# The last expert's way out: scattering through four row groups of the array, and a final norm straight from PSUM

## The chip, the cores and the metric

One Trainium2 chip, one of its NeuronCores. The metric is the time of one execution on the device in microseconds; each time below is the median of several executions. The engines that matter are TensorE (PE; PEld is its weight load), VectorE (DVE), ScalarE (ACT), GpSimd (POOL) and SyncE (SP), which issues nearly all DMAs.

## The reference

A two-layer trunk over x of 256 tokens x 1024 features in float32. Each layer is a mixer (a linear recurrence beside a stick-breaking attention) and then a channel mixer with a residual add: a dense SwiGLU in layer 0, and in layer 1 eight experts of width 3072, of which each token takes two. A norm closes the trunk. What the change touches is the end of layer 1:

```python
def swiglu(h, w_g, w_u, w_d):
    return (jax.nn.silu(h @ w_g) * (h @ w_u)) @ w_d

# moe_swiglu: each expert's rows, weighted by the token's gate, are added at the token's place
y = jnp.zeros_like(hf).at[row_tok].add(y_rows * row_gate[:, None])
...
x = x + moe_swiglu(h, router_w[j], moe_w_gate[j], moe_w_up[j], moe_w_down[j])
return rms_norm(x, final_norm)      # x / sqrt(mean(x^2) + 1e-6) * final_norm
```

## The kernel before

x stays in SBUF as two tiles `xs[0]` and `xs[1]` of 128 tokens x 1024. The experts run one after another (`order`, `run`), each with room for `n` tiles of 32 tokens: three tiles (96 tokens) for the five experts with the most tokens, two for the others. The last expert in the order has three. A product (`Expert.product`) reads its weights in four slabs of 1 MB, and holds the tokens stationary: an output tile of 32 tokens x 1024 columns is computed as four column groups of the array, 32 columns each, so that the quarter `q` of the 1024 output columns lands on PSUM partitions `32q` to `32q+32`. A tile is thus 128 partitions x 256, and two tiles share a PSUM bank. Products are `g`, `u` and `d` (gate, up, down), each cut in three (`ES`); the order for the last expert ends g2, u2, d1, d2.

Rows of an expert come from x and go back to it through a 0/1 matrix (`oh`, tokens x slots). `turn_one_hot` turns it by two bf16 transposes in the product u2. After d2, `rows` copies each 32x256 piece from PSUM to its place in `y` (slots x 1024), `scatter` multiplies by the turned one-hot (96 slots in the rows of the array), and VectorE adds the result, times the gate, to `xs`. For the last expert this is done in three rounds over the columns (`THIRDS`: 512, 256, 256), and `Final.square` follows each round with ScalarE's sum of squares, so that the norm's statistics grow with x. `Final.finish` then makes the two reciprocal roots on GpSimd (lines 260, 261), scales each half of each token block (ScalarE line 1148, VectorE line 1149), and SP stores the four halves of 256 KB (lines 1150, 1151).

While this stretch is made, `order_as_written` keeps PE, DVE and ACT in the order of the text; POOL and SP are ordered by the scheduler. PSUM accesses of two engines to one bank are kept apart by semaphores.

Behind it stand two branches (lines 1239, 1240), one behind the other, for an expert that has more tokens than its room: each engine loads one number (line 1238) and jumps over a body with a loop over all experts. With these inputs neither body runs. The arm that is taken instead waits for what is under way on each engine, SP for its stores. Line 1337 is the program's end: SP's last waits and the barrier of all engines.

Of the kernel before, what the change touches and what calls it, by code (L numbers as in the profile page):

```python
# [7 lines left out]
F32 = mybir.dt.float32  # L8
# [44 lines left out]
def trunk(ctx, tc, x, mix_norm, w_in, conv_w, conv_b, w_rgate, b_rgate, w_igate, b_igate, lru_lambda,  # L53
# [860 lines left out]
    def moe(j, pool, psum, route):  # L914
# [77 lines left out]
        class Expert:  # L992
# [15 lines left out]
            def product(self, name, s, hooks):  # L1008
# [4 lines left out]
                for i in range(4):  # L1013
                    w = load([self.source(name, s)[:, 2 * i:2 * i + 2]])
                    for kk in range(2):
                        k = 2 * i + kk
                        first = k == 0 and (name != "d" or s == 0)
                        last = k == KC - 1 and (name != "d" or s == ES - 1)
                        for t in range(self.n):
                            if name == "d":  # L1020
                                sh = self.turned[s][:, t, kk, i]
                            else:
                                sh = self.xT[:, k, t * 32:(t + 1) * 32]
                            for q in range(QN):
                                PE.matmul(outs[t][q * 32:(q + 1) * 32], sh,  # L1025
                                          w[:, kk * D + q * QW:kk * D + (q + 1) * QW],
                                          start=first and t % 2 == 0,
                                          stop=last and (t % 2 == 1 or t == self.n - 1))
# [56 lines left out]
            def turn_one_hot(self, exact=False):  # L1085
# [7 lines left out]
                if exact:  # L1093
                    self.y = pool.tile([CAP, D], F32, tag="yhi", name="yx", bufs=1)[:c32]
                else:
                    self.yhi = pool.tile([CAP, D], F32R, tag="yhi", name="yhi", bufs=1)[:c32]
                    self.ylo = pool.tile([CAP, D], F32R, name="ylo", bufs=1)[:c32]
# [25 lines left out]
        THIRDS = ((0, 512), (512, 768), (768, 1024))  # L1123

        class Final:
# [8 lines left out]
            def square(self, n, tb):  # L1134
                lo, hi = THIRDS[n]
                ss, x, y = self.ss[tb], xs[tb], self.ys[tb]
                ACT.activation(y[:, 512:512 + hi - lo], x[:, lo:hi], AF.Square, scale=1.0 / 32.0,
                               accum_out=ss[:, n:n + 1])
                if n == 0:
                    POOL.tensor_tensor(y[:, :512], x[:, :512], self.grow[0], op=OP.mult)  # L1140
                if n == 1:
                    POOL.tensor_tensor(ss[:, 0:1], ss[:, 0:1], ss[:, 1:2], op=OP.add)

            def finish(self):
                rs = [rstd_of_halves(ss[:, 0:1], ss[:, 2:3]) for ss in self.ss]
                for tb in range(NB):
                    y0, y1 = self.ys[tb][:, :512], self.ys[tb][:, 512:]
                    ACT.activation(y0, y0, AF.Copy, scale=rs[tb])
                    DVE.scalar_tensor_tensor(y1, xs[tb][:, 512:], rs[tb], self.grow[1], op0=OP.mult, op1=OP.mult)
                    nc.sync.dma_start(out[0, tb * P:(tb + 1) * P, :512], y0)  # L1150
                    nc.sync.dma_start(out[0, tb * P:(tb + 1) * P, 512:], y1)
# [15 lines left out]
        def run(jobs, whole):  # L1167

            waiting = []

            def hooks(name, job, s, i):
# [5 lines left out]
                if name == "u" and s == ES - 1:  # L1177
                    if i == 0 and after:
                        after.one_hot()
                    if i == 2:  # L1180
                        job.turn_one_hot(after is None)
# [9 lines left out]
            final = None  # L1191
            for name, job, s in order(jobs):
                if name == "d" and s == ES - 1 and job is jobs[-1] and whole:
                    final = Final()
# [3 lines left out]
                job.product(name, s, hooks)  # L1198
# [9 lines left out]
            for n, (lo, hi) in enumerate(THIRDS):  # L1208
                for q in range(lo // QW, hi // QW):
                    job.rows(q)  # L1210
                for tb in range(NB):
                    job.scatter(tb, lo, hi)
                if whole:
# [127 lines left out]
```

## Time and profile before

| | |
|---|---|
| median of 3 executions | 1204.24 us (1203.52 to 1204.24) |
| profiled execution, its own time | 1204.76 us |
| span of the profiled execution, first to last instruction | 1202.9 us |
| busy share of the span | PE 96%, PEld 65%, DVE 33%, ACT 27%, POOL 7% |
| mean granted TensorE clock | 0.986 of full speed |
| last down product, last instruction starts | 1176.6 us |
| first and last store issue on SP | 1190.94 us, 1194.34 us |

All times in rows are counted from the span's first instruction. A matmul in float32 is two instructions. The ends of matmuls are modelled and they overlap, so a busy TensorE is not one at its peak, and the pace of a stream is read from the starts. "Idle before, releaser" says how long an engine stood before an instruction and what ended that.

### The profile page before, as it was taken

What the parts mean: (1) busy time and instruction counts of PE and PEld (TensorE: products, weight loads), DVE (VectorE), ACT (ScalarE), POOL (GpSimd) and SP (SyncE); (2) the same over time, 40 slices, a digit from 0 to 9 for tenths busy, and PEclk for the clock granted to TensorE, in tenths of its full rate; (3) what the DMA queues carried; (4) which work ended last, traced back from release to release, by engine and by line L of the source; (5) the groups of instructions that cost most, each with busy time, mean ns of one, the idle gap of its engine ahead of it and who ended that gap; (6) DMA issues with size and microseconds to landing.
All of it is one profiled execution on the core that took longest, in us unless ns stands there. A gap on an engine that the chain in (4) does not pass through costs nothing.

```text
span 1202.9 us, 33274 instructions
## 1 busy us (share of the span) xinstructions
PE 1150.5 (96%) x15027; PEld 786.8 (65%) x15027; DVE 393.0 (33%) x668; ACT 320.6 (27%) x552; POOL 87.5 (7%) x142
## 2 busy tenths in 40 slices
PE   7989999999999979999999999999999999999993
PEld 5978888888898756665565665555565665555651
DVE  5796654555688662002002002011003002002002
ACT  6664644444467551001001001010001001001002
POOL 3154000000003600000000000000000000000001
PEclk9999999999999989999999999999999999999996
DMA  9933655555362289999999999999999999999971
GB/s 279 335 105 105 210 186 198 176 181 185 134 218 89 89 326 409 408 407 407 407 408 407 408 408 408 407 406 405 404 403 404 403 407 399 408 402 403 406 284 40
DMA packets 117032, 375.13 MB, mean 312 GB/s; under 512 B 6032, under 2 KB 22528, under 8 KB 116880
## 3 DMA queue, kind: packets, MB, share of 16 engines
q1 hardware_dynamic: 116592, 372.33, 80.9%
q8 instruction: 122, 2.00, 0.7%
q0 software_dynamic: 288, 0.56, 0.2%
q14 instruction: 30, 0.25, 0.1%
HBM read 371.81 MB, written 1.05 MB: 310 GB/s over the span
## 4 chain that ended last, share of the span: by engine, by line
PE 57%; DMA 3%; DVE 3%; ACT 1%; issue 0%; POOL 0%; POOLq 0%; ACTq 0%
PE d L1025 17%; PE g L1025 17%; PE u L1025 16%; DMA raw<-in_moe_w_up 2%; DMA raw<-in_moe_w_down 2%; PE gat L1076 1%; DVE ylo L1111 1%; PE at L1053 1%; ACT yhi L1110 1%; PE sc L1118 1%; PE sc L1119 1%; PE sc L1116 0%; PE po L148 0%; PE po L147 0%; PE po L149 0%
## 5 line engine op out<-in xcount | busy, mean ns | idle before, releaser
L1025 PE MATMUL u<-raw,xT 128*32 128x256 f32 x4032 | 228.0, 380 | 0.6 <-DMA raw<-in_moe_w_up 0.6
L1025 PE MATMUL g<-raw,xT 128*32 128x256 f32 x4032 | 227.2, 380 | 0.0
L1025 PE MATMUL d<-raw,aT 128*32 128x256 f32 x4032 | 225.5, 379 | 1.3 <-DMA raw<-in_moe_w_down 1.3
L1025 PEld LDWEIGHTS u<-raw,xT 128*32 128x32 f32 x4032 | 127.9, 110 | 89.4 <-issue 5.5
L1025 PEld LDWEIGHTS d<-raw,aT 128*32 128x32 f32 x4032 | 129.2, 110 | 87.3 <-DMA raw<-in_moe_w_down 2.7
L1025 PEld LDWEIGHTS g<-raw,xT 128*32 128x32 f32 x4032 | 127.6, 110 | 87.9 <-issue 6.7
L133 DVE TENSOR_TENSOR wlo<-raw,whi 128x1024 fp32r<-128x1024 f32 x96 | 116.8, 1224 | 93.1 <-ACT whi L132 93.0
L132 ACT ACTIVATE whi<-raw 128x1024 fp32r<-128x1024 f32 x96 | 100.6, 1060 | 106.9 <-PE u L149 38.6
L1058 ACT ACTIVATE aT<-at 128x512 f32<-128x512 f32 x24 | 14.3, 598 | 370.9 <-PE at L1053 354.8
L1040 DVE TENSOR_TENSOR act<-act,u 128x512 f32<-128x512 f32 (+1 forms) x39 | 21.4, 581 | 207.6 <-PE u L1025 146.6
L147 PE MATMUL proj<-hhi,whi 128*128 128x256 f32 x256 | 76.3, 298 | 0.0
L1111 DVE TENSOR_TENSOR ylo<-d,yhi 32x256 fp32r<-32x256 f32 x72 | 30.2, 419 | 133.7 <-ACT yhi L1110 132.9
L148 PE MATMUL proj<-hlo,whi 128*128 128x256 f32 x256 | 73.5, 287 | 0.0
L149 PE MATMUL proj<-hhi,wlo 128*128 128x256 f32 x256 | 73.4, 287 | 0.0
L1140 POOL TENSOR_TENSOR raw<-x,raw 128x512 f32<-128x512 f32 x2 | 2.5, 1270 | 741.5 <-DVE x L1120 741.5
L147 PEld LDWEIGHTS proj<-hhi,whi 128*128 128x128 f32 x256 | 50.1, 196 | 2.0 <-issue 1.5
L148 PEld LDWEIGHTS proj<-hlo,whi 128*128 128x128 f32 x256 | 50.2, 196 | 0.2
L149 PEld LDWEIGHTS proj<-hhi,wlo 128*128 128x128 f32 x256 | 50.1, 196 | 0.0
L1110 ACT ACTIVATE yhi<-d 32x256 fp32r<-32x256 f32 x72 | 27.0, 376 | 78.1 <-PE d L1025 58.3
L1034 ACT ACTIVATE act<-g 128x512 f32<-128x512 f32 (+1 forms) x39 | 18.4, 513 | 98.8 <-PE g L1025 98.8
L143 DVE TENSOR_TENSOR wlo<-raw,whi 128x1024 fp32r<-128x1024 f32 x32 | 39.9, 1254 | 5.2 <-ACT whi L142 5.1
L142 ACT ACTIVATE whi<-raw 128x1024 fp32r<-128x1024 f32 x32 | 33.8, 1061 | 20.7 <-PE proj L148 10.7
(259 smaller groups left out, 1344.2 us busy)
## 6 DMA issues: line engine op xcount, KB each, us to landing
raw<-in_moe_w_gate SPq DMA_DIRECT2D x96, 1024.0 KB, 19.3
raw<-in_moe_w_up SPq DMA_DIRECT2D x96, 1024.0 KB, 18.4
raw<-in_moe_w_down SPq DMA_DIRECT2D x96, 1024.0 KB, 18.5
raw<-in_w_in SPq DMA_DIRECT2D x18, 1024.0 KB, 5.3
raw<-in_dense_w_gate SPq DMA_DIRECT2D x12, 1024.0 KB, 5.2
raw<-in_dense_w_up SPq DMA_DIRECT2D x12, 1024.0 KB, 5.2
raw<-in_dense_w_down SPq DMA_DIRECT2D x12, 1024.0 KB, 5.0
raw<-in_w_out SPq DMA_DIRECT2D x8, 1024.0 KB, 11.4
```

The lines of the kernel that those rows point to most:

```text
L132: ACT.activation(hi, r, AF.Copy)
L133: DVE.tensor_tensor(lo, r, hi.bitcast(F32), op=OP.subtract)
L142: ACT.activation(h3, r, AF.Copy)
L143: DVE.tensor_tensor(lo.rearrange("p (k f) -> p k f", f=P), r, h3.bitcast(F32), op=OP.subtract)
L147: PE.matmul(ps, sh, mh, start=start, stop=False)
L148: PE.matmul(ps, sh, ml, start=False, stop=False)
L149: PE.matmul(ps, sl, mh, start=False, stop=stop)
L1025: PE.matmul(outs[t][q * 32:(q + 1) * 32], sh, w[:, kk * D + q * QW:kk * D + (q + 1) * QW], start=first and t % 2 == 0, stop=last and (t % ...
L1034: ACT.activation(a[:, at], b, AF.Silu)
L1040: DVE.tensor_tensor(a[:, at], a[:, at], b, op=OP.mult)
L1110: ACT.activation(self.yhi[to, w], ps, AF.Copy)
L1111: DVE.tensor_tensor(self.ylo[to, w], ps, self.yhi[to, w].bitcast(F32), op=OP.subtract)
```

## The change

Six things are changed at the end of layer 1, for the last expert alone.

- `spread` replaces the last expert's `turn_one_hot`: VectorE multiplies the one-hot by the gate and repeats each tile's 32 slots four times; six f32 transposes (three for each token block) give a stationary matrix of 128 rows, in which each group of 32 rows holds one tile's slots. ScalarE and VectorE copy it out of PSUM.
- `carry` adds, after each of the four slabs of the last down product, two identity matmuls that put one quarter of the columns of x (both token blocks, 256 columns each) into a PSUM bank of its own; the four banks are those of the products g and u.
- In the last slab of the last product the matmuls are ordered by tile (`by_tile`).
- `Final.scatter` copies each tile as it stands (three copies of 128x256), and multiplies with 32 rows of the array at a time: row group `q` adds quarter `q` of the columns to bank `q`, onto x. That is 3 tiles x 2 blocks x 4 quarters, 24 calls.
- `Final.of_banks` makes the norm out of these banks: ScalarE's sum of squares for the first token block, VectorE's `bn_stats` and `bn_aggr` for the second, the roots on GpSimd, the products on VectorE and ScalarE, two stores issued by SP and two by ScalarE. Behind these, x is copied back from the banks to `xs`, for the branch.
- The second branch goes into the body of the first (`others`), so that one branch is met; the norm for this rare case is `of_rows`.

The diff, cut to its core:

```diff
--- before.py
+++ after.py
@@ -1005,27 +1005,28 @@
-            def product(self, name, s, hooks):
+            def product(self, name, s, hooks, by_tile=False):
...
                     w = load([self.source(name, s)[:, 2 * i:2 * i + 2]])
-                    for kk in range(2):
+                    steps = [(kk, t) for kk in range(2) for t in range(self.n)]
+                    for kk, t in sorted(steps, key=lambda step: step[1]) if by_tile and i == 3 else steps:
...
-        THIRDS = ((0, 512), (512, 768), (768, 1024))
+            def spread(self):
+                og = pool.tile([P, D], F32, tag="ylo", name="og", bufs=1)[:, :NB * self.n * P]
+                og = og.rearrange("p (b t q n) -> p b t q n", b=NB, t=self.n, q=QN)
+                self.ohT = pool.tile([P, KC * CAP], F32, tag="xT", name="ogT", bufs=2)
+                for tb in range(NB):
+                    oh = self.oh[:, tb].rearrange("p (t n) -> p t n", n=32)
+                    DVE.tensor_scalar(og[:, tb], oh[:, :, None, :].to_broadcast([P, self.n, QN, 32]),
+                                      self.scales[:, tb, self.e:self.e + 1], None, op0=OP.mult)
+                for tb in range(NB):
+                    pt = bank("w", "ogt")
+                    for t in range(self.n):
+                        PE.transpose(pt[:, t * P:(t + 1) * P], og[:, tb, t].rearrange("p q n -> p (q n)"), ident)
+                    to = self.ohT[:, tb * TT * P:(tb * TT + self.n) * P]
+                    if tb:
+                        DVE.tensor_copy(to, pt[:, :self.n * P])
+                    else:
+                        ACT.activation(to, pt[:, :self.n * P], AF.Copy)
         class Final:
@@ -1131,24 +1149,82 @@
                 self.ys = [ys[:, tb * D:(tb + 1) * D] for tb in range(NB)]
                 self.ss = [const.tile([P, 4], F32, tag="ssf", name="ssf", bufs=2) for _ in range(NB)]
-            def square(self, n, tb):
-                lo, hi = THIRDS[n]
-                ss, x, y = self.ss[tb], xs[tb], self.ys[tb]
-                ACT.activation(y[:, 512:512 + hi - lo], x[:, lo:hi], AF.Square, scale=1.0 / 32.0,
-                               accum_out=ss[:, n:n + 1])
-                if n == 0:
-                    POOL.tensor_tensor(y[:, :512], x[:, :512], self.grow[0], op=OP.mult)
-                if n == 1:
-                    POOL.tensor_tensor(ss[:, 0:1], ss[:, 0:1], ss[:, 1:2], op=OP.add)
-            def finish(self):
-                rs = [rstd_of_halves(ss[:, 0:1], ss[:, 2:3]) for ss in self.ss]
+            def carry(self, q):
+                if q == 0:
+                    self.banks = [bank(tag, "xf") for tag in "gguu"]
                 for tb in range(NB):
-                    y0, y1 = self.ys[tb][:, :512], self.ys[tb][:, 512:]
-                    ACT.activation(y0, y0, AF.Copy, scale=rs[tb])
-                    DVE.scalar_tensor_tensor(y1, xs[tb][:, 512:], rs[tb], self.grow[1], op0=OP.mult, op1=OP.mult)
-                    nc.sync.dma_start(out[0, tb * P:(tb + 1) * P, :512], y0)
-                    nc.sync.dma_start(out[0, tb * P:(tb + 1) * P, 512:], y1)
+                    PE.matmul(self.quarter(tb, q), ident, xs[tb][:, q * QW:(q + 1) * QW], start=tb == 0, stop=False)
+            def quarter(self, tb, q):
+                return self.banks[q][:, tb * QW:(tb + 1) * QW]
+            def scatter(self, job):
+                y = pool.tile([P, D], F32, tag="yhi", name="yl", bufs=1)
+                for t in range(job.n):
+                    to, ps = y[:, t * QW:(t + 1) * QW], job.banks["d"][1][t]
+                    if t % 2:
+                        DVE.tensor_copy(to, ps)
+                    else:
+                        ACT.activation(to, ps, AF.Copy)
+                for t in range(job.n):
+                    for tb in range(NB):
+                        for q in range(QN):
+                            lot, at = slice(q * 32, (q + 1) * 32), (tb * TT + t) * P
+                            PE.matmul(self.quarter(tb, q), job.ohT[lot, at:at + P], y[lot, t * QW:(t + 1) * QW],
+                                      start=False, stop=t == job.n - 1 and tb == NB - 1)
+            def store(self, tb, hf, engine):
+                w = slice(hf * 512, (hf + 1) * 512)
+                engine.dma_start(out[0, tb * P:(tb + 1) * P, w], self.ys[tb][:, w])
+            def of_banks(self):
+                ss, y = self.ss, [[self.ys[tb][:, q * QW:(q + 1) * QW] for q in range(QN)] for tb in range(NB)]
+                grow = [self.grow[q // 2][:, q % 2 * QW:(q % 2 + 1) * QW] for q in range(QN)]
+                bn = pool.tile([P, QN * 6 + 2], F32, name="bn", bufs=1)
+                for q in range(QN):
+                    ACT.activation(y[0][q], self.quarter(0, q), AF.Square, scale=1.0 / 32.0,
+                                   accum_out=ss[0][:, q:q + 1])
+                for q in range(QN):
+                    DVE.bn_stats(bn[:, q * 6:(q + 1) * 6], self.quarter(1, q))
+                mean, var = (bn[:, i:i + 1] for i in (QN * 6, QN * 6 + 1))
+                DVE.bn_aggr(bn[:, QN * 6:], bn[:, :QN * 6])
+                DVE.scalar_tensor_tensor(ss[1][:, 0:1], mean, mean, var, op0=OP.mult, op1=OP.add)
+                r1 = rstd_of(ss[1][:, 0:1], 1, "rs")
+                POOL.tensor_scalar(ss[0][:, 0:1], ss[0][:, 0:1], ss[0][:, 1:2], ss[0][:, 2:3], op0=OP.add, op1=OP.add)
+                r0 = rstd_of_halves(ss[0][:, 0:1], ss[0][:, 3:4])
+                for q in range(3):
+                    DVE.tensor_tensor(y[0][q], self.quarter(0, q), grow[q], op=OP.mult)
+                for q in range(QN):
+                    DVE.scalar_tensor_tensor(y[1][q], self.quarter(1, q), r1, grow[q], op0=OP.mult, op1=OP.mult)
+                    if q % 2:
+                        self.store(1, q // 2, nc.sync)
+                for q in range(3):
+                    ACT.activation(y[0][q], y[0][q], AF.Copy, scale=r0)
+                    if q % 2:
+                        self.store(0, q // 2, ACT)
+                DVE.scalar_tensor_tensor(y[0][3], self.quarter(0, 3), r0, grow[3], op0=OP.mult, op1=OP.mult)
+                self.store(0, 1, ACT)
+                for q in range(QN):
+                    DVE.tensor_copy(xs[1][:, q * QW:(q + 1) * QW], self.quarter(1, q))
+                    ACT.activation(xs[0][:, q * QW:(q + 1) * QW], self.quarter(0, q), AF.Copy)
+            def of_rows(self):
+                for tb in range(NB):
+                    for hf in range(2):
+                        w = slice(hf * 512, (hf + 1) * 512)
+                        ACT.activation(self.ys[tb][:, w], xs[tb][:, w], AF.Square, scale=1.0 / 32.0,
+                                       accum_out=self.ss[tb][:, hf:hf + 1])
+                    r = rstd_of_halves(self.ss[tb][:, 0:1], self.ss[tb][:, 1:2])
+                    for hf in range(2):
+                        w = slice(hf * 512, (hf + 1) * 512)
+                        DVE.scalar_tensor_tensor(self.ys[tb][:, w], xs[tb][:, w], r, self.grow[hf],
+                                                 op0=OP.mult, op1=OP.mult)
+                        self.store(tb, hf, nc.sync)
...
                     if i == 2:
-                        job.turn_one_hot(after is None)
+                        if whole and after is None:
+                            job.spread()
+                        else:
+                            job.turn_one_hot(after is None)
+                if name == "d" and s == ES - 1 and after is None and whole:
+                    finals[0].carry(i)
-            final = None
             for name, job, s in order(jobs):
-                if name == "d" and s == ES - 1 and job is jobs[-1] and whole:
-                    final = Final()
+                closing = name == "d" and s == ES - 1 and job is jobs[-1] and whole
+                if closing:
+                    finals.append(Final())
                 if name == "d" and s not in job.turned:
                     done, n = waiting.pop(0)
                     done.turn(n)
-                job.product(name, s, hooks)
+                job.product(name, s, hooks, closing)
                 if name == "g":
                     job.gate(s)
                 elif name == "u":
@@ -1205,16 +1286,15 @@
                     for q in range(QN):
                         job.rows(q)
             job = jobs[-1]
-            for n, (lo, hi) in enumerate(THIRDS):
-                for q in range(lo // QW, hi // QW):
+            if whole:
+                finals[0].scatter(job)
+                finals[0].of_banks()
+            else:
+                for q in range(QN):
                     job.rows(q)
                 for tb in range(NB):
-                    job.scatter(tb, lo, hi)
-                if whole:
-                    for tb in range(NB):
-                        final.square(n, tb)
-            if whole:
-                final.finish()
+                    for hf in range(2):
+                        job.scatter(tb, hf * 512, hf * 512 + 512)
...
-        for taken in range(0, SEQ - 32 * min(TILES), CAP):
+        def others(taken):
             with tc.If(n_most > taken):
                 if not taken:
                     for tb in range(NB):
@@ -1253,11 +1334,12 @@
                         DVE.tensor_copy(shift, to)
                         DVE.tensor_copy(to[:, :, :E - 1], shift[:, :, 1:])
                         DVE.tensor_copy(to[:, :, E - 1:], shift[:, :, :1])
-                final = Final()
-                for n in range(3):
-                    for tb in range(NB):
-                        final.square(n, tb)
-                final.finish()
+                if taken + CAP < SEQ - 32 * min(TILES):
+                    others(taken + CAP)
+                if not taken:
+                    Final().of_rows()
+        others(0)
```

## Rows read from the trace of the kernel before

**Rows 1.** The page: busy time, share of the span, instructions of TensorE.
```profile
PE 1150.5 (96%) x15027; PEld 786.8 (65%) x15027; DVE 393.0 (33%) x668; ACT 320.6 (27%) x552; POOL 87.5 (7%) x142
```

**Rows 2.** Chain that ended last, 1140 to 1177 us: start, length, what.
```profile
1152.37 0.24 PE oht L1091 x2
...
1160.52 0.81 PE at L1053 x6
1161.32 15.29 PE d L1025 x280
```

**Rows 3.** Windows: length, busy by engine (instructions), granted clock, DMA share, GB/s.
```profile
1161.00:1177.00 16.00, 16.00 (x291) 9.34 (x289) 0.42 (x1) 0.96 (x2) 0.00 (x0) 1.00 0.25 100
1183.00:1190.00 7.00, 4.11 (x8) 2.35 (x8) 2.79 (x6) 2.42 (x9) 1.13 (x4) 0.50 0.01 2
```

**Rows 4.** Chain that ended last, 1176 to 1203 us.
```profile
1178.48 1.97 PE sc L1116 x4
...
1183.04 2.06 PE sc L1116 x4
...
1185.70 0.51 ACT raw L1137 x2
...
1189.17 0.31 POOL rstdf L260
...
1189.56 0.56 POOL rstdf L261
```

**Rows 5.** Timeline of TensorE in three stretches: start, length, what.
```profile
74.31 0.87 PE L472 MATMUL av<-wT,v 128*64 128x256 f32 x8
...
352.82 0.60 PE L402 MATMUL gates<-xc,bd 128*128 128x256 f32 x2
353.25 0.59 PE L403 MATMUL gates<-xc,bd 128*128 128x256 f32 x2
...
431.23 1.91 PE L820 MATMUL logit<-hT,scratch 128*8 128x128 f32 x16
```

**Rows 6.** Groups by line and form, 1176 to 1192 us.
```profile
L1106 DVE COPY yx<-d 32x256 f32<-32x256 f32 x6 | 2.5, 420 | 16.6 <-ACT yx L1108 16.5
...
L1120 DVE SCALAR_TENSOR_TENSOR x<-sc,sgate,x 128x256 f32<-128x256 f32 x4 | 1.9, 484 | 3.5 <-PE sc L1116 3.5
```

**Rows 7.** Groups by line and form on VectorE, 40 to 420 us.
```profile
L495 DVE TENSOR_TENSOR xp<-proj,rB 128x256 f32<-128x256 f32 x8 | 3.3, 413 | 0.0
...
L489 DVE COPY ms<-rb 128x2 f32<-128x2 f32 x2 | 0.3, 153 | 0.0
```

**Rows 8.** Issues of the output: ns least/median/most, first and last start.
```profile
L1151 SPq DMA_DIRECT2D out<-raw x2: 365/780/1196, 1190.9 to 1194.3; - x2
L1150 SPq DMA_DIRECT2D out<-raw x2: 378/1064/1749, 1191.4 to 1192.5; - x2
```

**Rows 9.** Line 1240, the branches: each engine's queue.
```profile
L1240 PEldq COMPARE_BRANCH  x2: 3907/4439/4971, 1187.4 to 1191.5; - x2
...
L1240 ACTq COMPARE_BRANCH  x2: 45/48/50, 1192.6 to 1192.8; - x2
...
L1240 ACTq EVENT_SEMAPHORE  x2: 17/17/17, 1192.7 to 1193.3; - x2
L1240 DVEq EVENT_SEMAPHORE  x2: 21/21/21, 1193.2 to 1196.9; - x2
L1240 SPq COMPARE_BRANCH  x2: 45/49/53, 1195.6 to 1198.3; - x2
```

**Rows 10.** Line 1240 between 1197.5 and 1198.5 us.
```profile
L1240 SPq EVENT_SEMAPHORE  x6: 17/17/17, 1197.9 to 1198.2; - x6
```

**Rows 11.** Line 1240 between 1200 and 1201.3 us.
```profile
L1240 SPq EVENT_SEMAPHORE  x8: 17/17/17, 1200.8 to 1201.2; - x8
```

**Rows 12.** Line 1337, the end, from 1201.3 us.
```profile
L1337 SPq EVENT_SEMAPHORE  x14: 17/28/28, 1201.3 to 1202.9; - x14
```

More of the change, by code (lines that the diff above doesn't have):

```diff
@@ L1018, in product @@
                         last = k == KC - 1 and (name != "d" or s == ES - 1)
[L1019 to L1028, printed above, removed]
+                        if name == "d":
+                            sh = self.turned[s][:, t, kk, i]
+                        else:
+                            sh = self.xT[:, k, t * 32:(t + 1) * 32]
+                        for q in range(QN):
+                            PE.matmul(outs[t][q * 32:(q + 1) * 32], sh,
+                                      w[:, kk * D + q * QW:kk * D + (q + 1) * QW],
+                                      start=first and t % 2 == 0,
+                                      stop=last and (t % 2 == 1 or t == self.n - 1))
                     hooks(name, self, s, i)
@@ L1093, in turn_one_hot @@
                 if exact:
-                    self.y = pool.tile([CAP, D], F32, tag="yhi", name="yx", bufs=1)[:c32]
+                    self.y = pool.tile([P, D], F32, tag="yhi", name="yx", bufs=1)[:c32]
                 else:
-                    self.yhi = pool.tile([CAP, D], F32R, tag="yhi", name="yhi", bufs=1)[:c32]
-                    self.ylo = pool.tile([CAP, D], F32R, name="ylo", bufs=1)[:c32]
+                    self.yhi = pool.tile([P, D], F32R, tag="yhi", name="yhi", bufs=1)[:c32]
+                    self.ylo = pool.tile([P, D], F32R, tag="ylo", name="ylo", bufs=1)[:c32]
             def rows(self, q):
@@ L1167, in run @@
         def run(jobs, whole):
-            waiting = []
+            waiting, finals = [], []
             def hooks(name, job, s, i):
@@ L1207, in run @@
             job = jobs[-1]
-            for n, (lo, hi) in enumerate(THIRDS):
-                for q in range(lo // QW, hi // QW):
+            if whole:
+                finals[0].scatter(job)
+                finals[0].of_banks()
+            else:
+                for q in range(QN):
                     job.rows(q)
                 for tb in range(NB):
-                    job.scatter(tb, lo, hi)
-                if whole:
-                    for tb in range(NB):
-                        final.square(n, tb)
-            if whole:
-                final.finish()
+                    for hf in range(2):
+                        job.scatter(tb, hf * 512, hf * 512 + 512)
         every = (moe_w_gate, moe_w_up, moe_w_down)
```

## The prediction

> **What bounds the kernel now.** I read the page first, then the chain of waits, stretch by stretch, backwards from the end. On the page TensorE is busy 96% of the span [rows 1], so two questions decide about any edit: does it add work to TensorE while TensorE is the last to be ready, and what happens in the stretch where TensorE is not. The chain over the last expert [rows 2] is TensorE alone: the last two down products run from 1155.3 to 1176.6 us, broken by six transposes, and 280 column-group instructions take 15.29 us, 0.0546 us each. In that stretch the clock is full and DMA is busy a quarter of the time [rows 3]: the weights are in, so whatever TensorE gets on top there moves the end one for one.
>
> From 1176.6 us the picture turns. [...] The part after that belongs to the stores: the four issues on SP's one queue run from 1190.94 to 1195.54, the third and fourth costing 1.75 and 1.20 us where the first two cost 0.37 and 0.38 [rows 8]; SP then meets the first skipped branch at 1195.6, in whose arm it waits for each store (the last at 1197.9), branches again at 1198.3, is in the second arm at 1200.8 and ends at 1202.9 [rows 9 to 12]. So the tail that the change rewrites is 1176.6 to 1202.9: 26.3 us.
>
> **What it adds ahead of that tail.** `spread` puts six 128x128 f32 transposes where two bf16 ones stood. Six of these cost 0.81 in a stream of column-group matmuls, the two cost 0.24 [rows 2]: +0.57. Its two VectorE products (the gated one-hot, 128x384) need only the one-hot and the gates, both long there, and VectorE has nothing to do between products; its two copies lie under the next product. If VectorE came late, TensorE would stand for at most one such product, about 0.5.
>
> `carry` puts x into four PSUM banks with two identity matmuls of 128x256 f32 after each of the last product's four slabs. Each call is two instructions; four such run 0.43 apart per call [rows 5], so a slab's pair costs 0.86, plus the change between column groups and the whole array: six transposes take 0.81, where sixteen f32 matmuls of 128 columns take 1.91 with the last one's end [rows 2, 5], some 0.11 each, so the two changes cost about 0.15. Three carries before the last slab: 3.0. The last product then starts its last instruction at 1176.6 + 0.57 + 3.0 = 1180.2 instead of 1176.6. This is the price of the change, and nothing hides it.
>
> **What it removes.** Twelve 32x256 copies in three rounds become three 128x256 copies. A copy costs 0.42 for 32 partitions [rows 6], and 128x256 products out of PSUM cost 0.41 [rows 7], so the width is free. By the tile order of the last slab the first bank (two of the three tiles) is complete 16 instructions, 0.9 us, early: ScalarE and VectorE copy it one after the other (they share the bank, as before), and the third tile is copied (0.4) under the fourth carry (1.0). So TensorE waits for no copy; scattering can start at 1180.2 + 1.1 = 1181.3, plus a change to row groups that the trace doesn't show: 0 to 0.3, I take 0.15.
>
> The scatter is 24 calls, 48 instructions of 256 columns. Nothing in this trace uses row groups. The nearest row is the column groups, 0.0546 each, four at a time: 2.6 us. The other bound is one at a time, 0.215 each: 10.3. I take the near end, since two-column-group matmuls with other operands also run side by side (eight instructions of 256 and 128 columns in 0.87, [rows 5]), and 0.3 for the last one to drain: done at 1184.4, the clock still full because TensorE never stands. [...]
>
> Then the norm out of PSUM. ScalarE squares four quarters of the first token block: the old squares of 128x256 stood 0.51 apart with their accumulator reads [rows 4]: 2.05, to 1186.5. VectorE takes the second block from the same four banks, one bank behind ScalarE, so its last `bn_stats` ends one instruction later. The trace has no `bn_stats`: not under the 0.15 of a two-element copy [rows 7], hardly over two passes, 0.9; I take 0.45 by the other 128x256 forms. `bn_aggr` and the small combine: 0.15 to 0.25 each. VectorE's statistics are there at 1187.4, and GpSimd's pair (0.31 and 0.56, with its waits 1.12, [rows 4]) gives r1 at 1188.5. r0 needs one sum more on GpSimd: 1188.1 if it goes first, 1189.9 if it is queued behind r1.
>
> VectorE is the engine that the rest waits for: three products 0.41 each [rows 7] to 1188.6, four fused ones at 0.48 [rows 6] to 1190.6, one more for the first block's last quarter to 1191.1. ScalarE scales three quarters (0.4 each) from r0 on and issues its two stores between them; the last store leaves at about 1191.3 (1191.1 to 1191.7). Before, it left at 1194.3. The stores wait behind nothing else: two on SP, two on ScalarE's queue. The second one there holds ScalarE's four copies back into x, which nobody but the branch needs.
>
> **Stores and end.** Before, the last store was seen 3.5 us after its issue began (1194.3 to 1197.9), of which 1.2 was the issue [rows 8, 10]. SP's first two issues cost 0.37, and each queue has only two now: 2.7 to 3.5, so 1194.0 to 1194.8; I take 1194.4. From the last landing SP needs the rest of its arm (0.4), its final waits and the barrier (1201.3 to 1202.9, 1.6, [rows 12]): 2.0. The second branch, 1198.3 to 1201.3, is gone: -3.0. That gives 1196.4. ScalarE's own way to the end is of the same length: its four copies to 1193.5, the register load of line 1238 and the branch to about 1194.3, then its arm and the barrier. I add 0.2 for that: 1196.6 against 1202.9, a gain of 6.3 us. In parts: -3.0 by the store's start, -0.4 by its landing, -3.0 by the branch, +0.2 for ScalarE (rounded). The profiled execution's own time is 1204.76, its span and 1.86 more; less 6.3 that is 1198.5. The median shown is 0.52 below it, so I forecast **1197.9**.
>
> **Rivals.** *Row groups that run one after another* (the other side). The trace shows side-by-side work for column groups alone, and 96 rows of the array took as long as any at the lower clock (four instructions in 2.06, [rows 4]). At 0.215 each the scatter is 7.7 longer: 1205.6, no change. If each weight load shows as well (some 0.11) it is 0.33 an instruction, 15.6: 1211, slower; from 0.235 an instruction on it is slower by over 0.2%. Against it: each row group has its own PSUM bank and its own 32 partitions. *Weight loads as the limit*: 48 loads of 128 columns at the 0.11 that separates the f32 matmuls of 128 columns are 5.3, so +2.7: 1200.6.
>
> *The longer jump.* The one branch skips both bodies. Of the old jumps some were dear: TensorE's took 3.9 and 5.0 us, VectorE's second arm came 3.6 after its first (1193.2 to 1196.9), SP's 2.4, while ScalarE's two took 0.7 in all (1192.6 to 1193.3) [rows 9, 11]. TensorE's lies early now and SP's under the landing. But ScalarE and VectorE copy x back before they branch, at about 1194; if either fetches for 3.6 there, the barrier comes at 1198 and the span ends near 1199: 1200.3, still faster. That both old arms on ScalarE were cheap speaks against it, VectorE's second for it. [...]
>
> *Carried x for nothing*: if the norm's chain were no shorter than the old third round, only the branch would be won (3.0), less 3.6 of TensorE work: 1204.8. The old way from the last product to the last store's issue took 17.7 (1176.6 to 1194.3); mine takes 11.1 (1180.2 to 1191.3), so 6.6 us would have to come up that no row shows.
>
> **How the numbers follow.** As forecast 0.60 (1196 to 1199.5 by itself); longer jump 0.19; weight loads or two groups at a time 0.07; serial, loads hidden, or the norm longer 0.07; serial and exposed 0.07. 0.2% (2.4 us) is about what a measurement can tell from no change. Faster: the first three, less 0.02 of the second that could pass 1201.8: 0.84; same 0.09; slower 0.07. All terms at their best (changes of array shape at nothing, -0.6; combine, -0.2; landing after 2.3, -0.8; ScalarE's 0.2) give 1196.1, and carries may be cheaper still; the longer jump and the weight loads give 1200.3 and 1200.6, with a microsecond for the norm 1201.6. Range 1195.6 to 1201.8.
>
> **What would show it.** The last down product ending 3.6 us later, with four gaps of about a microsecond; the 48 scatter instructions inside 3 us at a granted clock of 1.00, starts in fours; four ScalarE squares 0.51 apart with VectorE one behind; last store issued near 1191; one branch an engine. Wrong if scatter starts stand 0.2 apart, if a branch wait of 3 us ends last, or if `bn_stats` takes over a microsecond.

## The result, and the profile after

The changed kernel takes 1196.85 us (median of 4 runs, 1195.41 to 1197.96) where the kernel before took 1203.88 beside it (1201.95 to 1204.24): a ratio of 0.9947, 95% interval 0.9933 to 0.9961. The forecast was 1197.9. The profiled execution took 1197.96 with a span of 1196.2, 6.7 us less than before.

Page of the changed kernel, TensorE's line and the two queues of the kind `instruction`, called the first and the second code queue below:
```profile
PE 1152.6 (96%) x15083; PEld 790.1 (66%) x15083; DVE 393.5 (33%) x675; ACT 319.0 (27%) x550; POOL 84.2 (7%) x139
...
q8 instruction: 120, 1.97, 0.7%
...
q14 instruction: 29, 0.24, 0.1%
```
TensorE does 2.1 us more than in [rows 1] and the kernel is faster: the gain lies where TensorE is not the limit.

The chain that ended last, from the spread on (start, length, what):
```profile
1152.16 0.81 PE ogt L1136 x6
...
1160.88 0.81 PE at L1054 x6
1161.68 7.91 PE d L1026 x144
1169.59 1.06 PE xf L1158 x4
1170.65 2.73 PE d L1026 x48
...
1180.95 1.06 PE xf L1158 x4
1182.02 2.88 PE xf L1176 x48
1184.90 0.47 ACT raw L1189 x2
...
1185.39 1.54 DVE bn L1192 x4
...
1186.95 0.28 DVE bn L1194
...
1187.62 1.10 DVE raw L1200 x3
1188.72 0.38 DVEq L1318
...
1190.28 0.40 DVE raw L1209
...
1190.74 0.34 ACTq L1181
...
1191.13 1.28 ACT x L1213 x4
```
It reads as the prediction wrote it: product slabs with carries (L1158) between them, the scatter (L1176), one square, VectorE's four statistics one bank behind, its three and four products, the last store. The view follows the last instruction that counts as busy, ScalarE's copies back into x (L1213); landings, branch and barrier come behind it and are read from the rows below. The third round of copies, scatter and update [rows 4, 6] is gone.

Two windows of the changed kernel (columns as in [rows 3]):
```profile
1182.00:1184.50 2.50, 2.50 (x49) 2.31 (x48) 0.00 (x0) 0.00 (x0) 0.00 (x0) 1.00 0.00 0
...
1189.00:1192.00 3.00, 0.00 (x0) 0.00 (x0) 2.99 (x9) 1.43 (x5) 0.00 (x0) 0.61 0.71 257
```
The scatter runs wholly at the full clock, where the old one stood at 0.50 [rows 3]. The clock falls only after TensorE's work has ended: it is 1.00 from 1184.5 to 1189.0 too, and 0.61 from 1189.0 to 1192.0.

The stores, the branch and the end of the changed kernel (each issue's and each queue's instructions, ns least/median/most, first and last start):
```profile
L1181 ACTq DMA_DIRECT2D out<-raw x2: 339/360/381, 1189.1 to 1190.7; - x2
L1181 SPq DMA_DIRECT2D out<-raw x2: 361/364/366, 1189.5 to 1190.3; - x2
```
```profile
L1321 SPq EVENT_SEMAPHORE  x8: 17/17/17, 1193.9 to 1194.5; - x8
L1321 PEldq COMPARE_BRANCH  x1: 3520/3520/3520, 1184.0 to 1184.0; - x1
...
L1321 DVEq COMPARE_BRANCH  x1: 72/72/72, 1189.2 to 1189.2; - x1
L1321 SPq COMPARE_BRANCH  x1: 53/53/53, 1190.7 to 1190.7; - x1
L1321 DVEq EVENT_SEMAPHORE  x1: 21/21/21, 1192.0 to 1192.0; - x1
...
L1321 ACTq EVENT_SEMAPHORE  x1: 17/17/17, 1193.4 to 1193.4; - x1
```
No issue takes longer than 0.38 us, where two took 1.75 and 1.20 [rows 8]. One branch an engine; SP branches at 1190.7, is in its arm at 1193.9 (from the branch to the arm is called the jump below, here 3.2 us) and through its eight waits at 1194.5; VectorE and ScalarE are in theirs before it.

### The profile page after: what moved, and what is told of

Its sections match the earlier page's. It is cut to its first block, busy times and chain, and to the rows that moved or that the text cites. A ratio compares the mean times of both kernels' runs of the same rounds, so it can differ in the third digit from the quotient of the medians.

```text
span 1196.2 us, 33361 instructions
## 1 busy us (share of the span) xinstructions
PE 1152.6 (96%) x15083; PEld 790.1 (66%) x15083; DVE 393.5 (33%) x675; ACT 319.0 (27%) x550; POOL 84.2 (7%) x139
## 4 chain that ended last, share of the span: by engine, by line
PE 59%; DVE 3%; DMA 2%; ACT 1%; issue 0%; POOL 0%; DVEq 0%; ACTq 0%
PE g L1026 18%; PE d L1026 18%; PE u L1026 17%; DMA raw<-in_moe_w_up 2%; PE gat L1077 1%; DVE ylo L1112 1%; PE at L1054 1%; ACT yhi L1111 1%; PE sc L1119 1%; PE sc L1120 1%; PE xf L1158 0%; PE xf L1176 0%; PE po L148 0%; PE po L147 0%; PE po L149 0%
```

## The experiments

Where the last product starts moves by some microseconds from kernel to kernel (1158.0 to 1161.7), so besides the ratio the table has the **tail**: from the start of the last six transposes ahead of the last down product (timeline of TensorE) to the end of the span. Up to there all kernels do the same but for the spread, whose 0.57 us lie ahead of the tail and which before and e2 do not have; the change's 7.0 us on the tail are some 6.4 on the whole. One trace each, to 0.1 us.

| kernel | ratio to before, 95% | transposes | span | tail |
|---|---|---|---|---|
| before | 1 | 1160.45 | 1202.9 | 42.4 |
| changed | 0.9947 [0.9933, 0.9961] | 1160.81 | 1196.2 | 35.4 |
| e1 changed, again | 0.9951 [0.9938, 0.9965] | 1159.86 | 1195.2 | 35.3 |
| e2 one branch alone | 0.9970 [0.9957, 0.9982] | 1158.70 | 1197.7 | 39.0 |
| e3 two branches | 0.9981 [0.9972, 0.9991] | 1161.21 | 1200.6 | 39.4 |
| e4 one store queue | 0.9963 [0.9949, 0.9976] | 1160.37 | 1196.7 | 36.3 |
| e5 row groups apart | 1.0022 [1.0013, 1.0031] | 1158.10 | 1201.9 | 43.8 |
| e6 no carry | 0.9911 [0.9898, 0.9924] | 1161.65 | 1192.4 | 30.8 |
| e7 carries at the end | 0.9943 [0.9930, 0.9955] | 1160.96 | 1195.3 | 34.3 |
| e8 statistics from bank 2 | 0.9942 [0.9929, 0.9955] | 1158.83 | 1194.0 | 35.2 |
| e9 e7 and e8 | 0.9940 [0.9927, 0.9953] | 1159.63 | 1193.7 | 34.1 |
| e10 stores on ScalarE | 0.9954 [0.9941, 0.9967] | 1158.01 | 1193.8 | 35.8 |
| e11 e7, e8 and e10 | 0.9930 [0.9917, 0.9943] | 1158.72 | 1192.5 | 33.8 |
| e12 no copy back | 0.9952 [0.9938, 0.9967] | 1161.10 | 1196.9 | 35.8 |

**e1: the changed kernel again**, no edit.

> The changed kernel again, so that the others can be set against it in the same call. My theory: about 6.7 us under the kernel before (ratio near 0.9945), of which the last store's earlier start is 3.6, its landing 0.1 to 0.3, and the branch that is gone 3.0.

The tail repeats within 0.1 us, the ratio within its interval. A tail that differs by 0.3 or more is read as a difference below, a smaller one only with rows that show it. That limit rests on two traces, and in e12 the landing of the stores alone moves the tail by 0.4; so differences of 0.3 and 0.4 are weak evidence.

**e2: the kernel before with one branch, nothing else.**
```diff
-        for taken in range(0, SEQ - 32 * min(TILES), CAP):
+        def others(taken):
             with tc.If(n_most > taken):
...
+                if taken + CAP < SEQ - 32 * min(TILES):
+                    others(taken + CAP)
...
+        others(0)
```


> The kernel before with one part of the change alone: the second branch stands in the body of the first; scatter, norm and stores are the old ones. Branch worth its stretch on SP (the second jump 2.4 us and the second arm 0.5): 3.0 us less, ratio 0.9975, and the last store's issue stays near 1194.3. Rival, the jump over two bodies takes the place of the two: TensorE's, VectorE's or SP's arm comes so late that only 0 to 1 us is left, ratio 0.999 to 1.000. Second rival, the branch is the whole gain: ratio 0.9945.

Issues of the output in e2:
```profile
L1151 SPq DMA_DIRECT2D out<-raw x2: 365/519/673, 1189.2 to 1191.8; - x2
L1150 SPq DMA_DIRECT2D out<-raw x2: 377/665/953, 1189.7 to 1190.8; - x2
```
SP's part of the branch's line in e2, and SP's first two waits in its first arm in the kernel before:
```profile
L1240 SPq EVENT_SEMAPHORE  x8: 17/17/17, 1195.5 to 1196.0; - x8
...
L1240 SPq COMPARE_BRANCH  x1: 53/53/53, 1192.5 to 1192.5; - x1
```
```profile
L1240 SPq EVENT_SEMAPHORE  x2: 17/17/17, 1196.7 to 1197.3; - x2
```
The tail is 3.4 us shorter, the 3.0 of the second branch and 0.4 more. The same four issues on the same queue got shorter: the third and fourth cost 0.95 and 0.67 instead of 1.75 and 1.20 [rows 8], which had not been expected, and counted from the transposes SP meets its branch 1.3 us earlier. Only 0.4 of that is left at the end, because SP's one jump takes 3.0 us (1192.5 to 1195.5), where the old first one took 1.1 (1195.6 [rows 9] to 1196.7). The branch is half of the change's gain of 7.0 on this tail.

**e3: the changed kernel with two branches in a row.**
```diff
-        def others(taken):
+        for taken in range(0, SEQ - 32 * min(TILES), CAP):
             with tc.If(n_most > taken):
...
-                if not taken:
-                    Final().of_rows()
-        others(0)
+                Final().of_rows()
```


> The changed kernel with one part undone: the two branches stand one behind the other again, everything else as changed. If the branch's price is additive: 3.0 us over the changed kernel, ratio to the kernel before near 0.997, SP's second arm 2.4 to 3 us behind its second jump. Rival, with the stores earlier the second jump is hidden under the landing: under 1 us over the changed kernel, ratio near 0.995.

Issues of the output, and SP's part of the branch's line, in e3:
```profile
L1181 ACTq DMA_DIRECT2D out<-raw x2: 381/634/887, 1189.5 to 1191.1; - x2
L1181 SPq DMA_DIRECT2D out<-raw x2: 365/849/1333, 1189.9 to 1190.7; - x2
```
```profile
L1321 SPq EVENT_SEMAPHORE  x16: 17/17/17, 1193.7 to 1198.9; - x16
...
L1321 SPq COMPARE_BRANCH  x2: 45/49/53, 1192.1 to 1196.0; - x2
```
4.0 us come back: 3.0 from SP's second branch to the end of its second arm (1196.0 to 1198.9), and 1.0 by which its first waits end later. With them come back the long issues (1.33 and 0.89), now with two queues. So the second branch costs its own jump, and the stores are longer with it, in either kernel.

**e4: all four stores on SP.**
```diff
-                        self.store(0, q // 2, ACT)
+                        self.store(0, q // 2, nc.sync)
...
-                self.store(0, 1, ACT)
+                self.store(0, 1, nc.sync)
```


> The changed kernel with all four stores issued by SP. My theory (a third and fourth issue on one queue cost 1.75 and 1.20 us): last issue starts 1.3 to 1.8 later than in the changed kernel and the span ends 1.3 to 1.8 us later, ratio near 0.996. Rival (those long issues came from the second half of the old kernel's stores standing beside code that TensorE fetched for its two branches, not from the queue): each issue costs 0.37 and the end moves by 0 to 0.4, ratio near 0.9947.

Issues of the output, and SP's part of the branch's line, in e4:
```profile
L1181 SPq DMA_DIRECT2D out<-raw x4: 366/388/839, 1188.6 to 1190.5; - x4
```
```profile
L1321 SPq EVENT_SEMAPHORE  x8: 17/17/17, 1194.4 to 1195.0; - x8
...
L1321 SPq COMPARE_BRANCH  x1: 53/53/53, 1191.0 to 1191.0; - x1
```
0.9 us slower by the tail, but not for the expected reason: on one queue, with one branch, three of the four issues stay under 0.4. What costs is that SP's branch comes behind the last store (1191.0, counted from the transposes 0.7 later than in the changed kernel) and its jump of 3.4 us (to 1194.4) ends after the landings, the last of which the trace has at 1193.9. The second queue helps because it takes a store from ahead of SP's jump.

**e5: one row group after another.** The same 24 calls with the loop over row groups outside:
```diff
-                for t in range(job.n):
-                    for tb in range(NB):
-                        for q in range(QN):
+                for q in range(QN):
+                    for t in range(job.n):
+                        for tb in range(NB):
```


> The changed kernel with the same 48 scatter instructions in another order: all twelve of one row group, then those of the next, so that neighbours share a row group. If the row groups' side-by-side run is what makes the scatter short (48 starts in 2.5 us): 0.215 each, 10.3 in all, the scatter 7 to 7.7 us longer and the time at or above the kernel before, 1203.5 to 1204.5, ratio 1.000. Rival, TensorE finds work for idle row groups wherever it stands in its queue: the scatter stays under 4 us and the time near 1197.

Windows of e5, the scatter's line alone (length, PE busy, PEld busy, granted clock, DMA share, GB/s), and its piece in the chain:
```profile
1179.20:1182.00 2.80, 2.76 (x16) 2.49 (x17) 1.00 0.00 0
1182.00:1185.00 3.00, 3.00 (x16) 2.56 (x15) 0.71 0.00 0
1185.00:1188.00 3.00, 3.00 (x12) 2.56 (x11) 0.50 0.03 5
```
```profile
1179.31 12.35 PE xf L1176 x48
```
The order of the calls alone makes 12.35 us of 2.88, and the kernel slower than before. So it is the side-by-side running that pays. Neighbours in e5 share the row group and also the PSUM bank, since each row group adds to a bank of its own; which of the two keeps them apart, no run here shows. Of the 9.5 us more, 8.4 reach the end of the tail: the squares and statistics of three banks now run under the scatter. And not all is the order: the granted clock falls from 1.00 to 0.50 in the middle of it, while TensorE is busy without a gap with one row group at a time. No term of the prediction had that.

**e6: no carry.** The eight identity matmuls are left out and the scatter starts the banks, so x is missing from the sum:
```diff
-                for tb in range(NB):
-                    PE.matmul(self.quarter(tb, q), ident, xs[tb][:, q * QW:(q + 1) * QW], start=tb == 0, stop=False)
...
-                                      start=False, stop=...)
+                                      start=t == 0 and tb == 0, stop=...)
```


> The changed kernel without the eight identity matmuls: x is left out of the sum, the norm is taken over the last expert's share alone. It prices the carry. My theory: TensorE sets the pace there, so the end comes earlier by what the four carries take, four times 1.06 to 1.18 us: 4.3 to 4.7 under the changed kernel, ratio to the kernel before near 0.991. Rival, the weights' transfer or the copies set the pace behind it: 1 to 2 us.

The tail is 4.6 us shorter: that is the whole price of the carries. The changed chain shows it too: a carry takes 1.06, and the 48 instructions of the slab behind it 2.73, where they took 2.62 at 0.0546 [rows 2]; 1.17 each, 4.7 for four.

**e7: all four carries behind the last slab.**
```diff
-                    finals[0].carry(i)
+                    for q in range(QN) if i == 3 else ():
+                        finals[0].carry(q)
```


> The changed kernel with all four carries behind the last slab, in one go. The matmuls are the same; three times fewer changes between column groups and the whole array. If each change pair costs about 0.3 (1.39 us from the last column-group start to the next one around a carry, less 0.215, less four instructions of 0.215): 0.9 us under the changed kernel, ratio near 0.994. Rival, the change costs nothing and the gaps belong to the identity's weight load: same as the changed kernel within 0.2 us.

The chain of e7:
```profile
1169.96 7.55 PE d L1026 x140
1177.51 3.65 PE xf L1158 x16
1181.16 2.88 PE xf L1176 x48
```
Four carries in a row cost 3.65 (0.228 an instruction, against 0.215 in [rows 5]) instead of 4.7, and the tail is 1.1 shorter. So about 0.35 of each single carry is the change between column groups and the whole array and back; the prediction had 0.15. Nothing hides less: the copies of the last product still lie under the carries.

**e8: VectorE takes the banks in the order 2, 3, 0, 1**, so that it doesn't start behind ScalarE. Each `bn_stats` now also stands behind its square in the text, in one loop:
```diff
-                for q in range(QN):
-                    DVE.bn_stats(bn[:, q * 6:(q + 1) * 6], self.quarter(1, q))
+                    v = (q + 2) % QN
+                    DVE.bn_stats(bn[:, v * 6:(v + 1) * 6], self.quarter(1, v))
```


> The changed kernel with VectorE's statistics taken from banks 2, 3, 0, 1 while ScalarE squares banks 0, 1, 2, 3, each pair named together, so that they start on different banks. If sharing banks is what puts VectorE 0.51 us behind ScalarE: VectorE starts with ScalarE and the end comes 0.4 to 0.5 us earlier, ratio about 0.0004 lower than the changed kernel's. Rival, the chain runs by r0 and ScalarE's scaling instead: no change.

Timeline of e8:
```profile
1182.94 1.43 DVE L1192 BATCH_NORM_STATS2 bn<-xf 128x6 f32<-128x256 f32 x4 [3.92 <-PE xf L1176]
...
1185.09 0.56 POOL L261 TENSOR_TENSOR rstdf<-rstdf,half 128x1 f32<-128x1 f32 x1
...
1186.65 1.66 DVE L1202 SCALAR_TENSOR_TENSOR raw<-xf,rs,raw 128x256 f32<-128x256 f32 x4 [0.49 <-POOL rs L255]
```
The statistics start with ScalarE's squares and are ready half a microsecond earlier, but GpSimd is then still at r0 (to 1185.65) and r1 queues behind it: VectorE waits 0.49 for r1. The tail is shorter by 0.2 only. The wait moved from ScalarE's bank to GpSimd's queue.

**e9: e7 and e8 together** (both edits as above).

> The changed kernel with the four carries behind the last slab (e7) and the statistics started at the third bank (e8). Theory (two separate places of the chain: TensorE's changes of array shape, then VectorE's wait behind the squares): the two savings add, 1.04 us and 0.25 us measured from the last six transposes of the product to the end, so some 1.3 us less than the changed kernel, ratio to the kernel before near 0.9937. Rival: with the carries behind one another the copies of the last product hide less, so that the savings overlap and 1.0 us or less is left, ratio near 0.994.

1.3 us: the two savings add.

**e10: all four stores on ScalarE**, none on SP:
```diff
-                        self.store(1, q // 2, nc.sync)
...
-                    if q % 2:
-                        self.store(0, q // 2, ACT)
+                    if q == 1:
+                        self.store(0, 0, ACT)
+                self.store(1, 0, ACT)
+                self.store(1, 1, ACT)
```


> The changed kernel with all four stores issued by ScalarE, none by SP, so that SP meets the branch early and waits for the landings in its arm. Theory (SP's jump of 3.1 us behind its last store ends last, and not the landing): the branch starts before 1187, the last landing near 1194.1 sets the end; SP's arm is entered 0.4 us earlier at most and the end comes 0.2 to 0.4 us earlier than in the changed kernel. Rival (the landing ends last already): no gain, and up to 0.4 us lost if the issues queue up on ScalarE.

**e11: e7, e8 and e10 together.**

> The changed kernel with all three: carries behind the last slab, statistics from the third bank, all stores on ScalarE. Theory: savings add, 1.3 us of the first two and 0 to 0.4 us of the third, ratio to the kernel before 0.993 to 0.994. Rival: ScalarE, which now issues all stores and then copies x back and branches, becomes the engine that ends last, and the third takes back what the second gave: ratio no better than that of the first two alone.

Issues of the output in e10, then in e11, and SP's waits in its arm in e11:
```profile
L1181 ACTq DMA_DIRECT2D out<-raw x4: 381/390/1030, 1186.3 to 1188.4; - x4
```
```profile
L1181 ACTq DMA_DIRECT2D out<-raw x4: 338/360/382, 1185.5 to 1187.7; - x4
```
```profile
L1322 SPq EVENT_SEMAPHORE  x8: 17/17/17, 1189.1 to 1190.8; - x8
```
SP is now in its arm before the stores land (1189.1 in e11), so there the landing sets the end alone. In e10 that gained nothing: one issue on ScalarE took 1.03 and the tail is 0.4 longer. In e11, where no issue was long, the tail is 0.3 shorter than e9's, too little for the ratios to tell apart. In the changed kernel the two lie close together, the end of the jump at 1193.9 and the last landing, by the trace, at 1194.1; taking the jump away was worth 0.3 at most.

What makes one issue long in e10 and none in e11? The DMA view of narrow windows shows when packets of code start. Its line has packets, MB and the time that they took as a share of 16 engines. The first code queue in the kernel before (1191.9 to 1192.7, then 1192.5 to 1192.7), in e3 (1188.7 to 1189.4), in e10 (1186.2 to 1186.4) and in e11 (1185.4 to 1185.6):
```profile
q8 instruction: 2, 0.03, 32.3%
q8 instruction: 1, 0.02, 79.2%
```
```profile
q8 instruction: 2, 0.03, 33.6%
```
```profile
q8 instruction: 1, 0.02, 29.0%
```
```profile
q8 instruction: 1, 0.02, 29.0%
```
In the kernel before 32.3% of 16 engines in 0.8 us are 4.1 us for two packets, 2.5 of them (79.2% in 0.2 us) for the second: they start at 1192.0 and 1192.6 and are under way until 1193.6 and 1195.1. The two long issues start at 1192.5 and 1194.3, inside them. In e3 the two packets start at 1188.75 and 1189.3 and the later one is under way until 1191.4; the long issues start at 1190.7 and 1191.1. In e10 a packet of 0.93 us starts at 1186.25, and the long issue at 1186.79; in e11 a packet as long is over at 1186.39, and the second issue starts at 1186.44 and is short.

So it is in all fourteen traces: of their 56 issues of output eight take longer than 0.6 us, and each of these eight is the second or a later one on its queue and starts while a packet of code, of the first or the second code queue, is under way. Of the others that are not first on their queue, one alone starts so (e9, 0.04 us before the packet's end). A queue's first issue takes 0.36 to 0.38 even under a packet. What holds the later ones up is not shown, and no run moves the packets alone.

**e12: no copy back** of the eight quarters into x, which only the branch's body reads (it isn't entered here):
```diff
-                for q in range(QN):
-                    DVE.tensor_copy(xs[1][:, q * QW:(q + 1) * QW], self.quarter(1, q))
-                    ACT.activation(xs[0][:, q * QW:(q + 1) * QW], self.quarter(0, q), AF.Copy)
```


> The changed kernel without the eight copies of the sum from PSUM back into x, so that a second pass in the branch body would not find x (the body isn't entered with these inputs; this work is left out). Theory of the prediction's term of 0.2 us (ScalarE's own way to the end, its copies, its register load and its branch, is about as long as SP's): 0.2 us less than the changed kernel. Rival (SP's jump and arm end at 1194.5, ScalarE's arm is reached at 1193.4, VectorE's at 1192.0): nothing, the end moves by less than 0.1 us, and the copies cost nothing.

SP's waits in its arm in e12:
```profile
L1318 SPq EVENT_SEMAPHORE  x8: 17/17/17, 1194.2 to 1195.2; - x8
```
No gain: the ratio is that of the changed kernel. The tail is 0.4 longer in this one trace, where the eight waits take 1.0 us instead of 0.6: here the landing came last (1194.8 by the trace). The copies cost nothing that these runs can show: ScalarE is in its arm half a microsecond before SP with them (1193.4 and 1193.9 in the changed kernel).

## Why the prediction was right, point by point

The run of the changed kernel reaches the spread 0.21 us earlier than that of before (1152.16 against 1152.37 in [rows 2]). With 0.21 added to its times they stand beside the prediction's:

| step | predicted | measured |
|---|---|---|
| scatter starts | 1181.45 | 1182.2 |
| scatter over, first square | 1184.4 | 1185.1 |
| second block's statistics combined | 1187.4 | 1187.7 |
| last store issued | 1191.3 | 1190.95 |
| SP through its store waits | 1194.8 | 1194.7 |
| end of the span | 1196.6 | 1196.4 |

- **The price ahead of the tail was too small.** Spread: 0.81 for 0.24, the 0.57 of the prediction. Carries: four cost 4.6 to 4.7 (e6, the chain), where the prediction had 3.0 and 1.1. The identity matmuls were right; the change of array shape was mis-sized, about 0.35 a carry where 0.15 was taken (e7). So the scatter starts 0.75 late.
- **The scatter was right.** 48 instructions in 2.88 with the drain, predicted 2.9, at the full clock. The reason given for the clock, that TensorE never stands, no run shows: in e5 it never stands either and the clock falls to 0.50. The serial rival was the right one to fear: e5 is that rival built, and it ends slower than before.
- **The norm was too dear.** In the chain three products take 1.10 and the four fused ones 1.56 (1188.72 to 1190.28), so 0.37 and 0.39 each where 0.41 and 0.48 stood; the last one 0.40. ScalarE's squares start 0.35 to 0.38 apart (1184.88, 1185.26, 1185.62, 1185.97) instead of 0.51, and VectorE's four statistics take 1.54. The old rows' lengths of single instructions, for the squares with the accumulator read behind them, were taken for the distance between back-to-back ones, which overlap at their ends: the group of L1202 has a mean of 472 ns and a distance of 0.39. From the first square to the last issue that made 5.84 (1184.90 to 1190.74) of 6.9, and gave back more than the carries had cost too much. That the two misses cancel is luck: the last store's issue is 0.35 early by a start that was 0.75 late and a norm that was 1.1 shorter.
- **r0 first on GpSimd**: as hoped, and e8 shows why it is no free choice.
- **The stores: the size held, the reason did not.** The last landing came 3.4 us behind its issue's start (1190.74 to 1194.1) where 3.1 was taken. The prediction gave the long issues [rows 8] to the one SP queue. e4 has one queue and a single issue of 0.84; e2 shortens them on the same queue by taking a branch away, and e3 brings them back on two. They go with packets of code that are under way when an issue starts (e11), and e4's and e10's long ones show that this happens with one branch too. The first code queue has 122 packets with two branches (before, e3) and 120 with one (changed, e11), some 16 KB each (2.00 MB / 122); in the kernel before and in e3 two of them start as the stores go out, 0.5 and 1.1 us behind TensorE's second branch. That they are TensorE's code rests on this timing alone. The second code queue's packets are half that size (0.24 MB / 29).
- **The branch was half or more**: predicted 3.0 of 6.3; alone it is worth 3.4 of the tail's 7.0 (e2), put back it costs 4.0 (e3). The rest, 3 to 3.6, is x in PSUM with the four-way scatter and the norm from the banks, net of the carries and less the spread's 0.57 ahead of the tail. No run parts the new scatter from the new norm.
- **ScalarE's 0.2 was nothing**: it is in its arm at 1193.4, half a microsecond before SP, and e12 gains nothing.
- **The longer jump came on SP.** On ScalarE and VectorE, where the prediction feared it, it did not count: VectorE's takes 2.8 (1189.2 to 1192.0) and is hidden. But SP's one jump takes 3.2 (1190.7 to 1193.9; 3.0 in e2, 3.4 in e4) where the old first one took 1.1. The prediction had it under the landing and gave it no price. It ends 0.2 us before the last landing here, and behind it in e2 and e4: "a branch wait of 3 us ends last", a sign of being wrong, was missed narrowly. TensorE's jump takes 3.5 (3.52 us from 1184.0) and ScalarE's 0.5 (1192.9 to 1193.4), at the same branch; what makes a jump long, and that an engine fetches code in it, no run shows.

Four row groups side by side, at 256 columns of f32, take 0.052 an instruction (48 in 2.50) where one of the whole array at a time takes 0.215 [rows 5]: some 4 times.

## What to carry to other kernels

Ask at the end of a kernel what each skipped branch costs on every engine before tuning the arithmetic ahead of it: here one branch less was worth as much as the whole rewrite of scatter and norm (e2, 3.4 of 7.0 us). When small-K matmuls are spread over row groups, look to the order of the calls: here it was the gain (e5, 12.35 us against 2.88), with neighbours in different row groups and in different banks. Keep matmuls of one array shape together (e7, 1.1 us for moving a loop), and take the distance between back-to-back instructions from a chain, not from the mean of one (L1202, 0.39 us against 472 ns). The best version here is e11, ratio 0.9930; its interval overlaps the changed kernel's, but its tail is 1.6 us shorter.

## What the runs showed that was not expected

- The granted clock fell from 1.00 to 0.50 while TensorE was busy without a gap on one row group at a time (e5); the same 48 instructions with four row groups side by side ran at 1.00. They were over in 2.9 us, though, and the first 2.8 us of e5 ran at 1.00 too, so whether the arrangement or the length makes the difference is not shown.
- Store issues that are not the first on their queue take 0.67 to 1.75 us instead of 0.34 to 0.39 when they start under a packet of code, in eight cases of nine (e11).
- A wait taken from one engine can land in another's queue at nearly its full price (e8: 0.5 us won at the statistics, 0.49 lost at r1).
